# Unread products of the unit matrix on the tensor engine of a two-layer backbone kernel

## The chip, the cores and the metric

The kernel runs on one core of one Trainium2 chip. The metric is the device time of one execution in microseconds (us). The profile shows one execution in the same unit. Engines are named as the profile names them: PE is the tensor engine's product, PEld its weight load, DVE the vector engine, ACT the scalar engine, POOL the GpSimd engine and SP the engine that issues most of the DMAs.

## The reference

Two layers over 1024 latent tokens and 256 context tokens, width 1024, all in fp32. Cut to what matters here:

```python
def reference(x, c, ctx, c_ctx, mod_w, mod_b, norm_g, ...):
    x_lat, x_ctx = x, ctx
    for i in range(DEPTH):                      # DEPTH = 2
        h_lat = rms_norm(x_lat, norm_g[i]) * (1.0 + sc_l) + sh_l
        h_ctx = rms_norm(x_ctx, norm_g[i]) * (1.0 + sc_c) + sh_c
        if i % 2 == 0:   # global GQA with axial rotary | windowed GQA with a sink, each times silu(gate)
            y_lat, y_ctx = even_mixer(...)      # concat(oa * silu(ag), ob * silu(bg)) @ w_out
        else:            # conformer convolution | 2-D neighbourhood attention with a relative bias
            y_lat, y_ctx = odd_mixer(...)       # concat(oc, od * silu(dg)) @ w_out
        x_lat = x_lat + g_l * y_lat
        if i < DEPTH - 1:
            x_ctx = x_ctx + g_c * y_ctx
    return rms_norm(x_lat, final_g)
```

## The kernel before

An fp32 product is made of three products: each operand is split into a high part and a rest (`wh`, `wl`; `hh`, `hl`; `ph`, `pl`), and high times high, rest times high and high times rest are summed in PSUM (L318 to L320). The split's high part is a cast on ACT (L296), the rest a subtraction on POOL or DVE (L299).

Attention of both layers is written in one generator that works through groups of heads and queries, tile by tile. For each tile PE makes the scores `st` (L465, L469), ACT takes their exponential (L477), the split makes `ph` and `pl`, and `flush` adds three products to the group's sum `ov` (L409 to L411). After a group's last tile DVE transposes its denominators (L419), takes their reciprocal (L421), transposes back (L422) and multiplies `ov` by it into `y` (L631 in layer 0, L1367 in layer 1). The maxima that are needed ahead of the exponentials are products into `mx` (L588 in layer 0; L1342 and L1350 in layer 1), reduced on DVE. Layer 1 has 16 groups, eight heads by two halves, and its keys, biases and gates come by DMA.

A root mean square is made in steps by `rstd_steps`: products with ones give the sums of squares `trs` (L251), DVE copies them (`rbv`, L254), POOL makes a first guess (`nr`, L238), DVE refines it (`nt`, `nt`, `nr`, L239 to L241), and PE spreads it over the partitions (`bc`, L261).

The end of layer 1 goes in three parts: part 0 is the first half of the tokens, parts 1 and 2 are quarters. For each part `out1_end` makes the last output products `po` (L318 to L320, for parts 1 and 2 only the last of eight slices of the inner dimension), adds them to `x` (L1435) and sums the squares (ACT L1464, adds on DVE and POOL L1468, L1471); `c0`, `c1`, `c2` run `rstd_steps`; `f0`, `f1`, `f2` run `final_norm`, which copies `bc` (ACT L1479), multiplies `x` by it on DVE (L1486) or on POOL (L1484), and writes out. Part 0 is woven into the last attention groups; the rest runs in the order e1 c1 e2 f1 c2 f2.

PSUM has eight banks, given out by `bank(tag)`: two `pp`, two `mx`, two `st`, one `ov` and one `tr`. A new user of a bank waits until the last reader of the old content is done. What an engine runs in which order isn't written down: a scheduler sets it when the program is built, from priorities, dependencies and its own timeline of the engines. Each engine then runs its list strictly in order.

Of the kernel before, what the change touches and what calls it, by code (L numbers as in the profile page):

```python
# [18 lines left out]
P = 128  # L19
# [32 lines left out]
MWB, WRB = 2, 2  # L52
OHQ = 0
PCB = 3
MODP = ((), (1, 3, 6))
FL = (80, -98)
LAG = (0, 0, 6, 12)
# [30 lines left out]
def tile_kernel(ctx: ExitStack, tc: tile.TileContext, a, out):  # L88
    nc = tc.nc
    VE, SC, GP, PE, SY = nc.vector, nc.scalar, nc.gpsimd, nc.tensor, nc.sync  # L90
# [7 lines left out]
    solo = [True]  # L98
# [4 lines left out]
    def bank(tag, name):  # L103
        if tag == "pp" and solo[0]:
            turn[0] += 1
            tag = ("pp", "mx")[turn[0] // 2 % 2]
        return ps.tile([P, 512], F32, tag=tag, name=name, bufs=BUFS[tag])

    uid = [0]

    def nm(s):
        uid[0] += 1
        return f"{s}_{uid[0]}"
# [130 lines left out]
    def rstd_steps(pool, accs, n, tag, inv=1.0, tr="tr"):  # L244


        nb = n // P
        tr = bank(tr, nm("trs"))
        for b in range(nb):
            for k, acc in enumerate(accs):  # L250
                PE.matmul(tr[:, 2 * b : 2 * b + 2], acc[:, b * P : (b + 1) * P], ones, start=(k == 0),  # L251
                          stop=(k == len(accs) - 1))
        v = pool.tile([P, 8], F32, tag="rbv", name=nm("rbv"), bufs=2)
        VE.tensor_scalar(v[:, :nb], tr[:, 0 : 2 * nb].rearrange("p (b two) -> p b two", two=2)[:, :, 0],  # L254
                         inv, EPS, op0=ALU.mult, op1=ALU.add)
        r = newton_rsqrt(pool, v[:, :nb], nb, "rb")
        yield
        yield
        bc = bank(tag, nm("bc"))
        for b in range(nb):  # L260
            PE.matmul(bc[:, b * P : (b + 1) * P], r[:, b : b + 1].broadcast_to([P, P]), ident, start=True, stop=True)  # L261
        return bc
# [129 lines left out]
    def attn_gen(pool, groups, vshare, look, nexts=None):  # L392

        preps = [g.prep for g in groups]
        items = [(g, t) for g in groups for t in range(len(g.tiles))]
        pend = []
        cnt = [0]

        def flush():
            g, t, ph, pl = pend.pop(0)  # L400
            k, q0, n, _ = g.tiles[t]
            if t == 0:
                g.ov = bank("ov", nm("ov"))
                if g.load_v is not None:
                    g.load_v()
            V = g.v(k)
            last = t == len(g.tiles) - 1
            o = g.ov[:, q0 : q0 + n]
            PE.matmul(o, V[:, 64:192], ph[:, :n], start=(t == 0), stop=False)  # L409
            PE.matmul(g.ov[0:64, q0 : q0 + n], V[:, 0:64], ph[:, :n], start=False, stop=False)  # L410
            pvs.append(PE.matmul(o, V[:, 64:192], pl[:, :n], start=False, stop=(last and g.sink is None)))  # L411
            if last:
                if g.sink is not None:
                    PE.matmul(g.ov, g.skm(), g.QL[0:76, :], start=False, stop=True)
                r1 = pool.tile([P, 8, 32], F32, tag="r1", name=nm("r1"), bufs=1)
                r8 = pool.tile([P, 8], F32, tag="r8", name=nm("r8"), bufs=2)
                rb = pool.tile([P, 256], F32, tag="rb", name=nm("rb"), bufs=1)
                for e in range(2):
                    VE.transpose(r1[e * 64 : (e + 1) * 64].rearrange("p a b -> p (a b)")  # L419
                                 .rearrange("p (a q) -> p a q", a=2), g.den(g.ov[64:128, :], e))  # L420
                VE.reciprocal(r8, r1[:, :, 0])  # L421
                VE.transpose(rb, r8[:, :, None].broadcast_to([P, 8, 32]))  # L422
                g.finish(g.ov, rb)

        for p in preps[:2]:
            next(p)
            yield
        for _ in range(2):
            yield
        for p in preps[:2]:  # L430
            for n_, _ in enumerate(p):
                if n_ % 2:
                    yield
        work = []

        def prepare(x, n):

            while n and work and work[0][0] <= x:
                if next(work[0][1], work) is work:
                    work.pop(0)  # L440
                else:
                    n -= 1

        for gi, g in enumerate(groups):
            g.ids = [gi + 2] if gi + 2 < len(groups) else []
            if nexts is not None and gi in nexts:
                g.ids = nexts[gi]
        for g, t in items[:AHEAD]:
            g.ahead(t)
        for x, (g, t) in enumerate(items):  # L450
            if x + AHEAD < len(items):
                items[x + AHEAD][0].ahead(items[x + AHEAD][1])
            if t == 0:
                g.start()
                while any(p is g.prep for _, p in work):
                    prepare(len(items), 1)
                for k in g.ids:
                    next(preps[k])
                    work.append((x + LEAD[layer[0]], preps[k]))
            rate = g.rate * max(len(work), 1)  # L460
            k, q0, n, extra = g.tiles[t]
            KA, KB = g.k()
            st = bank("st", nm("st"))
            cs = slice(k * P, (k + 1) * P)
            sts.append(PE.matmul(st[:, :n], KA[:, cs], g.QH[:, q0 : q0 + n], start=True, stop=False))  # L465
            if not g.bias:
                for lhs, rhs in extra():
                    PE.matmul(st[:, :n], lhs, rhs, start=False, stop=False)
            PE.matmul(st[:, :n], KB[0:68, cs], g.QL[0:68, q0 : q0 + n], start=False, stop=True)  # L469
            ph = pool.tile([P, 512], F32R, tag="ph", name=nm("ph"), bufs=look + 1)  # L470
            pl = pool.tile([P, 512], F32R, tag="pl", name=nm("pl"), bufs=look + 1)
            pf = pool.tile([P, 512], F32, tag="pf" if layer[0] else "ost", name=nm("pf"), bufs=PFB)
            if g.bias and extra is not None:
                VE.tensor_tensor(pf[:, :n], st[:, :n], extra(), op=ALU.add)
                SC.activation(pf[:, :n], pf[:, :n], AF.Exp)
            else:
                SC.activation(pf[:, :n], st[:, :n], AF.Exp, scale=1.0 if g.bias else SCALE)  # L477
            cnt[0] += 1
            split(pf[:, :n], ph[:, :n], pl[:, :n], "s", "v" if cnt[0] % vshare == 0 else "g")
            pend.append((g, t, ph, pl))  # L480
            if t == len(g.tiles) // 2:
                g.gate()
            if t == len(g.tiles) - 1:
                g.last()
            prepare(x, rate // 2)
            yield
            if len(pend) > look:
                flush()
            prepare(x, rate - rate // 2)
            yield  # L490
        while pend:
            flush()
            yield
# [63 lines left out]
    def group0(u, qb):  # L557
# [12 lines left out]
        def maxes(QH, mp):  # L570
            KA = KAs[u]
            for i2 in range(2):
                mx = bank("mx", nm("mx"))
                for i in range(2):
                    hd = 2 * i2 + i
                    PE.matmul(mx[:, i * 256 : (i + 1) * 256], QH[:, hd * P : (hd + 1) * P], KA[:, 0:256],
                              start=True, stop=True)
                VE.tensor_reduce(mp[:, 2 * i2 : 2 * i2 + 2, 0], mx.rearrange("p (i k) -> p i k", i=2),
                                 axis=AX.X, op=ALU.max)
                yield  # L580
            if qb < 2:
                return
            for hd in range(4):
# [7 lines left out]
                else:  # L591
                    lo, hi = max(qb - 1, 2), min(qb + 2, 10)
                    n = (hi - lo) * P
                    mo = (lo - (qb - 1)) * P
                    mx = bank("mx", nm("mx"))
                    PE.matmul(mx[:, :n], q, KA[:, lo * P : hi * P], start=True, stop=True)
                    VE.tensor_tensor_reduce(out=mx[:, :n], in0=mx[:, :n], in1=bmask[:, mo : mo + n],
# [501 lines left out]
    with ExitStack():  # L1099
# [195 lines left out]
        def group1(gi, hd, hf):  # L1295
# [38 lines left out]
            def maxes(QH, mp):  # L1334
                KA = Ks[hd % len(Ks)][0]
                for b in (1, 2, 0, 3):
                    if b in (1, 0):
                        mx = bank("mx", nm("mx1"))
                        b0 = 1 - b
                        bb = (1, 2) if b else (0, 3)  # L1340
# [106 lines left out]

        def out1_end(k):

            hf, o, n = ENDS[k]  # L1450
            accs = []
            for e in range(DK):
                if k == 0:
                    if e % 2 == 0:
                        w = load_w(wp, a["od_wo"], e * P, 256, 256, WB, dks=range(4, 8))
                    yield from out1((4, 5, 6, 7), e, hf, *w, o, n)
                else:
                    yield from out1((7,), e, hf, *wend[e // 2], o, n)
                x = x2[hf][:, e, o : o + n]
                if k:  # L1460
                    sq = dpool.tile([P, 512], F32, tag="ph" if e in SQ else "pl", name=nm("sq2"), bufs=LOOK1 + 1)[:, :n]
# [172 lines left out]
```

## Time and profile before

| what | before |
|---|---|
| median of 3 runs | 1555.79 us (1553.47 to 1557.76) |
| the profiled execution | 1555.72 us, its span 1553.9 us |
| granted clock of PE, mean over the span | 0.967 |
| matmuls | 6984 |
| longest wait of PE at the end of layer 0 | 5.07 us, ended by `y` (DVE L631) |
| longest waits of PE at 1340 to 1360 us | 3.22 us, ended by a DMA, and 1.82 us |
| last `po` region of layer 1 begins | 1525.72 us |
| last work on DVE ends | 1549.2 us |

The table of the page shows each engine's busy time; the slices show it over the span in forty parts, with the granted clock below; the timeline lists single instructions with the idle time before them and what ended it. The prediction quotes the lines that it uses.

### The profile page before, as it was taken

What the parts mean: (1) busy time and instruction counts of PE and PEld (TensorE: products, weight loads), DVE (VectorE), ACT (ScalarE), POOL (GpSimd) and SP (SyncE); (2) the same over time, 40 slices, a digit from 0 to 9 for tenths busy, and PEclk for the clock granted to TensorE, in tenths of its full rate; (3) what the DMA queues carried; (4) which work ended last, traced back from release to release, by engine and by line L of the source; (5) the groups of instructions that cost most, each with busy time, mean ns of one, the idle gap of its engine ahead of it and who ended that gap; (6) DMA issues with size and microseconds to landing.
All of it is one profiled execution on the core that took longest, in us unless ns stands there. A gap on an engine that the chain in (4) does not pass through costs nothing.

```text
span 1553.9 us, 22052 instructions
## 1 busy us (share of the span) xinstructions
PE 1449.1 (93%) x6984; PEld 1172.3 (75%) x6984; DVE 1123.3 (72%) x2172; ACT 759.8 (49%) x1545; POOL 833.5 (54%) x762
## 2 busy tenths in 40 slices
PE   6989989999999989899999889999999999799995
PEld 1878868887789678678887668888787787687784
DVE  4998898689858666654577677999755457586776
ACT  2721354445454755565455555443434455545563
POOL 1561464555555676675455666664542443545574
PEclk9999999999999999999999999999999999899996
DMA  9548245423441124631111121213456888788623
GB/s 339 194 146 270 79 125 174 147 64 121 151 129 44 54 89 143 207 115 56 42 45 35 68 95 57 80 63 123 158 178 222 272 225 263 221 264 240 192 92 109
DMA packets 185614, 221.01 MB, mean 142 GB/s; under 512 B 17421, under 2 KB 139481, under 8 KB 185497
## 3 DMA queue, kind: packets, MB, share of 16 engines
q1 hardware_dynamic: 178832, 208.03, 43.1%
q10 hardware_dynamic: 6664, 11.57, 2.3%
q8 instruction: 55, 0.90, 0.2%
q14 instruction: 63, 0.51, 0.1%
HBM read 159.51 MB, written 60.03 MB: 141 GB/s over the span
## 4 chain that ended last, share of the span: by engine, by line
PE 67%; DVE 12%; DMA 11%; issue 3%; POOL 3%; ACT 2%; SPq 2%; DVEq 0%; ACTq 0%; POOLq 0%
PE p L320 6%; PE p L318 6%; PE p L319 6%; PE ov L409 4%; PE ov L410 4%; PE ov L411 4%; PE st L465 4%; PE po L318 4%; PE st L469 4%; PE po L319 4%; PE po L320 4%; PE pq L320 2%; PE pq L319 2%; PE pq L318 2%; DMA mw<-in_mod_w_dram 2%
## 5 line engine op out<-in xcount | busy, mean ns | idle before, releaser
L299 POOL TENSOR_TENSOR pl<-pf,ph 128x512 fp32r<-128x512 f32 (+4 forms) x321 | 399.9, 1258 | 270.7 <-ACT ph L296 218.9
L299 POOL TENSOR_TENSOR wl<-wr,wh 128x256 fp32r<-128x256 f32 (+2 forms) x256 | 197.7, 788 | 227.9 <-ACT wh L296 203.3
L477 ACT ACTIVATE pf<-st 128x512 f32<-128x512 f32 x284 | 166.2, 596 | 161.7 <-PE st L469 106.3
L296 ACT CAST ph<-pf 128x512 fp32r<-128x512 f32 (+4 forms) x364 | 209.2, 588 | 25.5 <-PE ov L410 17.6
L296 ACT CAST wh<-wr 128x256 fp32r<-128x256 f32 (+2 forms) x264 | 103.2, 404 | 172.2 <-DMA wr<-in_od_d_dram 39.3
L318 PE MATMUL p<-hh,wh 128*128 128x512 f32 x448 | 177.7, 399 | 3.7 <-DVE spk L299 1.4
L319 PE MATMUL p<-hl,wh 128*128 128x512 f32 x448 | 177.9, 398 | 0.2 <-POOL hl L299 0.2
L320 PE MATMUL p<-hh,wl 128*128 128x512 f32 x448 | 175.2, 399 | 0.1
L465 PE MATMUL st<-QH,KAt 128*128 128x512 f32 (+4 forms) x364 | 144.0, 397 | 19.8 <-ACT pf L477 16.5
L409 PE MATMUL ov<-ph,Vt 128*128 128x512 f32 (+4 forms) x364 | 143.6, 394 | 8.8 <-DVE y L631 6.4
L411 PE MATMUL ov<-pl,Vt 128*128 128x512 f32 (+4 forms) x364 | 143.7, 395 | 3.9 <-POOL pl L299 3.8
L410 PE MATMUL ov<-ph,Vt 128*64 128x512 f32 (+4 forms) x364 | 140.8, 387 | 0.0
L469 PE MATMUL st<-QL,KBt 68*128 68x512 f32 (+4 forms) x364 | 138.2, 388 | 0.8 <-DVE QL L388 0.7
L1116 DVE SCALAR_TENSOR_TENSOR cps<-U,taps,cps 128x512 f32<-128x512 f32 x184 | 124.3, 747 | 0.0
L589 DVE TENSOR_REDUCE mp<-mx 128x1 f32<-128x512 f32 x128 | 85.5, 682 | 33.5 <-PE mx L588 32.7
L219 DVE SCALAR_TENSOR_TENSOR macc<-mw,csil,macc 128x512 f32<-128x512 f32 x107 | 97.5, 929 | 14.0 <-DMA mw<-in_mod_w_dram 13.2
L318 PEld LDWEIGHTS p<-hh,wh 128*128 128x128 f32 x448 | 84.6, 189 | 24.5 <-DVE spk L299 1.6
L465 PEld LDWEIGHTS st<-QH,KAt 128*128 128x128 f32 x364 | 69.8, 192 | 42.5 <-ACT pf L477 25.3
L319 PEld LDWEIGHTS p<-hl,wh 128*128 128x128 f32 x448 | 84.6, 189 | 20.4 <-POOL hl L299 0.6
L320 PEld LDWEIGHTS p<-hh,wl 128*128 128x128 f32 x448 | 84.6, 189 | 20.3 <-POOL wl L299 1.0
L411 PEld LDWEIGHTS ov<-pl,Vt 128*128 128x128 f32 x364 | 71.1, 195 | 28.1 <-POOL pl L299 7.6
L409 PEld LDWEIGHTS ov<-ph,Vt 128*128 128x128 f32 x364 | 71.5, 196 | 24.3 <-issue 7.0
(277 smaller groups left out, 3518.4 us busy)
## 6 DMA issues: line engine op xcount, KB each, us to landing
mw<-in_mod_w_dram SPq DMA_DIRECT2D x34, 512.0 KB, 5.6
bs<-in_d_bs_dram SPq DMA_DIRECT2D x16, 832.0 KB, 7.3
Q<-qs SPq DMA_DIRECT2D x40, 256.0 KB, 2.7
QH<-Q SPq DMA_DIRECT2D x80, 128.0 KB, 2.7
bm<-in_d_bm_dram SPq DMA_DIRECT2D x16, 540.0 KB, 6.1
wr<-in_od_d_dram SPq DMA_DIRECT2D x64, 128.0 KB, 2.6
mw<-in_mod_w_dram SPq DMA_DIRECT2D x28, 256.0 KB, 3.1
wr<-in_ev_qkv_dram SPq DMA_DIRECT2D x32, 192.0 KB, 3.8
```

The lines of the kernel that those rows point to most:

```text
L296: SC.copy(hi, src)
L299: (GP if leng == "g" else VE).tensor_tensor(lo, src, hi.bitcast(F32), op=ALU.subtract)
L318: PE.matmul(o, lh, rh, start=first, stop=False)
L319: PE.matmul(o, lh, rl, start=False, stop=False)
L320: done[0] = PE.matmul(o, ll, rh, start=False, stop=last)
L409: PE.matmul(o, V[:, 64:192], ph[:, :n], start=(t == 0), stop=False)
L410: PE.matmul(g.ov[0:64, q0 : q0 + n], V[:, 0:64], ph[:, :n], start=False, stop=False)
L411: pvs.append(PE.matmul(o, V[:, 64:192], pl[:, :n], start=False, stop=(last and g.sink is None)))
L465: sts.append(PE.matmul(st[:, :n], KA[:, cs], g.QH[:, q0 : q0 + n], start=True, stop=False))
L469: PE.matmul(st[:, :n], KB[0:68, cs], g.QL[0:68, q0 : q0 + n], start=False, stop=True)
L477: SC.activation(pf[:, :n], st[:, :n], AF.Exp, scale=1.0 if g.bias else SCALE)
L1116: VE.scalar_tensor_tensor(pc, uc, w, pc, op0=ALU.mult, op1=ALU.add)
```

## The change

A table `WARM` says ahead of which instruction of a kind how many products are put. Counters go over the tiles' `st`, over the `flush` calls (`ov` ahead of the first product, `pl` ahead of the third), and over the maxima. `turn_over(count, tag)` takes a fresh bank of the given tag and issues `count` products of the unit matrix with itself, 128x512, which nobody reads. From the end of layer 1 on (`ending`), `rstd_steps` has 4 products ahead of its sums for part 0 (`solo` is not yet set), 8 for the others in the bank `ov`, and 6 ahead of `bc`; part 2 of `out1_end` has two for each of its eight slices of output.

```diff
+WARM = {"st": {297: 6, 299: 6}, "ma": {}, "mb": {}, "ov": {243: 18, 251: 6}, "pl": {251: 10}, "m1": {1: 6, 25: 5, 33: 8, 53: 5}}
...
+    seen, ending = {}, [False]
+
+    def warm(kind, n=1):
+
+        seen[kind] = seen.get(kind, 0) + n
+        count = sum(WARM[kind].get(k, 0) for k in range(seen[kind] - n + 1, seen[kind] + 1))
+        turn_over(count)
+
+    def turn_over(count, tag="tr"):
+
+        if count:
+            uid[0] -= 1
+            tr = bank(tag, nm("wm"))
+            for _ in range(count):
+                PE.matmul(tr.rearrange("p (a b) -> p a b", a=4), identr, identr[:, None, :].broadcast_to([P, 4, P]),
+                          start=True, stop=True)
...
+        if ending[0] and not solo[0]:
+            turn_over(4, "tr")
+        elif ending[0]:
+            turn_over(8, "ov")
         tr = bank(tr, nm("trs"))
...
         bc = bank(tag, nm("bc"))
+        if ending[0]:
+            turn_over(6, "tr")
...
             o = g.ov[:, q0 : q0 + n]
+            warm("ov")
             PE.matmul(o, V[:, 64:192], ph[:, :n], start=(t == 0), stop=False)
             PE.matmul(g.ov[0:64, q0 : q0 + n], V[:, 0:64], ph[:, :n], start=False, stop=False)
+            warm("pl")
             pvs.append(PE.matmul(o, V[:, 64:192], pl[:, :n], start=False, stop=(last and g.sink is None)))
...
+            warm("st")
             st = bank("st", nm("st"))
...
                     if b in (1, 0):
+                        warm("m1", 2)
                         mx = bank("mx", nm("mx1"))
...
         def out1_end(k):
+            ending[0] = True
...
                     yield from out1((7,), e, hf, *wend[e // 2], o, n)
+                if k == 2:
+                    turn_over(2, "ov")
```

(The kinds `ma` and `mb`, maxima of layer 0, have calls of the same form and no entries.) 124 products are added, and no instruction of the computation is taken away. The scheduler builds a new order with them. Up to the end of layer 0 the lists of all engines are the same.

At the end of layer 0, PE's list before has the last product of one group (`ov_9297`, tile `pl_9470`) and the first of the next (`ov_9583`) with two pairs of scores between and ahead:

```order
L410 MATMUL ov_9297<-ph_9469,Vt_1259 64x512
L465 MATMUL st_9524<-QH_8863,KAt_5707 128x512 [waits Activation_49]
L469 MATMUL st_9524<-QL_8864,KBt_1258 128x512
L411 MATMUL ov_9297<-pl_9470,Vt_1259 128x512 [waits Pool_49]
L465 MATMUL st_9561<-QH_8863,KAt_5707 128x512 [waits Activation_49]
L469 MATMUL st_9561<-QL_8864,KBt_1258 128x512
L409 MATMUL ov_9583<-ph_9492,Vt_1259 128x512 [waits DVE_49,PE_49]
```

With the change PE's list has there (from behind the same `ov_9297<-ph_9469`; `wm` are the added products):

```order
L124 MATMUL wm_9584<-ident 128x512 x15
L492 MATMUL st_9524<-QH_8863,KAt_5707 128x512 [waits Activation_49]
L496 MATMUL st_9524<-QL_8864,KBt_1258 128x512
L124 MATMUL wm_9584<-ident 128x512
L437 MATMUL ov_9297<-pl_9470,Vt_1259 128x512 [waits Pool_49]
L124 MATMUL wm_9584<-ident 128x512
L492 MATMUL st_9561<-QH_8863,KAt_5707 128x512 [waits Activation_49]
L496 MATMUL st_9561<-QL_8864,KBt_1258 128x512
```

```order
L124 MATMUL wm_9704<-ident 128x512 x4
L492 MATMUL st_9628<-QH_8863,KAt_5707 128x512 [waits Activation_49]
L496 MATMUL st_9628<-QL_8864,KBt_1258 128x512
L124 MATMUL wm_9713<-ident 128x512 [waits PE_49]
L124 MATMUL wm_9713<-ident 128x512 x9
L434 MATMUL ov_9583<-ph_9492,Vt_1259 128x512 [waits DVE_49]
```

Seventeen products now lie ahead of `pl_9470`, seventeen more and two further pairs of scores (`st_9606` and `st_9628`) between it and the next group's first `ov`.

At the end of layer 1, PE's list before has, behind the last group's last product, the spreading `bc` of part 0 and the first `po` of part 1:

```order
L411 MATMUL ov_16094<-pl_16247,Vt_12386 128x512 [waits Pool_49]
L261 MATMUL bc_16336<-ident,nr_16327 128x128 [waits DVE_49]
L261 MATMUL bc_16336<-ident,nr_16327 128x128 x3
L318 MATMUL po_4150_16402<-od_3594_14463,wh_16380 128x256 [waits Activation_49]
L318 MATMUL po_4152_16409<-od_3594_14463,wh_16380 128x256
```

and with the change (`wm_16555` is in the bank of `ov`, and its wait for DVE is that for `y`, which reads `ov_16173`):

```order
L273 MATMUL trs_16400<-ones,sq_4067_16178 128x2
L124 MATMUL wm_16555<-ident 128x512 [waits DVE_49,PE_49]
L124 MATMUL wm_16555<-ident 128x512 x7
L124 MATMUL wm_16421<-ident 128x512 [waits DVE_49]
L124 MATMUL wm_16421<-ident 128x512 x5
L342 MATMUL po_4150_16493<-od_3594_14536,wh_16471 128x256 [waits Activation_49]
L342 MATMUL po_4152_16500<-od_3594_14536,wh_16471 128x256
L124 MATMUL wm_16592<-ident 128x512 [waits PE_49]
```

Fourteen products lie ahead of the first `po`, and `bc` has gone behind the first two slices of output. The pairs of part 2 stand between the slices, and its `po` mix with those of part 1.

POOL's last rows before: the adds of squares, then the `nr` of parts 1 and 2, then the closing multiplications of parts 1 and 2.

```order
L1468 TENSOR_TENSOR sq_4172_16485<-sq_4172_16485,sq_4184_16531 128x256 [waits Activation_49,Pool_49]
L238 TENSOR_TENSOR nr_16471<-rbv_16469,mhalf 128x2 [waits DVE_49]
L238 TENSOR_TENSOR nr_16566<-rbv_16564,mhalf 128x2 [waits DVE_49]
L1484 TENSOR_TENSOR x_3593_14462<-x_3593_14462,bcs_16543 128x256 [waits Activation_49]
L1484 TENSOR_TENSOR x_3593_14462<-x_3593_14462,bcs_16543 128x256 x3
```

With the change:

```order
L256 TENSOR_TENSOR nr_16571<-rbv_16569,mhalf 128x2 [waits DVE_49]
L1502 TENSOR_TENSOR sq_4172_16595<-sq_4172_16595,sq_4184_16659 128x256 [waits Activation_49,Pool_49]
L1518 TENSOR_TENSOR x_3593_14535<-x_3593_14535,bcs_16674 128x256 [waits Activation_49]
L1518 TENSOR_TENSOR x_3593_14535<-x_3593_14535,bcs_16674 128x256 x3
L256 TENSOR_TENSOR nr_16706<-rbv_16704,mhalf 128x2 [waits DVE_49]
```

The `nr` of part 2 has gone from ahead of the four multiplications of part 1 to behind them.

More of the change, by code (lines that the diff above doesn't have):

```diff
@@ L572, in maxes @@
             for i2 in range(2):
+                warm("ma", 2)
                 mx = bank("mx", nm("mx"))
@@ L594, in maxes @@
                     mo = (lo - (qb - 1)) * P
+                    warm("mb")
                     mx = bank("mx", nm("mx"))
```

## The prediction

> **What bounds the kernel now.** The page comes first: which engine is busy, how that and the granted clock of the tensor engine (PE) lie over the span, and what the chain that ended last is made of.
>
> ```profile
> PE 1449.1 (93%) x6984; PEld 1172.3 (75%) x6984; DVE 1123.3 (72%) x2172; ACT 759.8 (49%) x1545; POOL 833.5 (54%) x762
> PE   6989989999999989899999889999999999799995
> PEclk9999999999999999999999999999999999899996
> PE 67%; DVE 12%; DMA 11%; issue 3%; POOL 3%; ACT 2%; SPq 2%; DVEq 0%; ACTq 0%; POOLq 0%
> ```
>
> PE is the bound of nearly the whole span, at nearly full clock; what a product on it costs depends on whether PE has a hole at that place. So the second view is the table of stretches, from the place of the first added product on (columns: length, busy time of PE, weight loads, DVE, ACT and POOL with their counts, granted clock, DMA share, GB/s).
>
> ```profile
> 880.00:900.00 20.00, 13.53 (x51) 9.30 (x49) 12.42 (x21) 13.26 (x24) 12.25 (x11) 0.83 0.01 3
> 920.00:1300.00 380.00, 373.94 (x1773) 304.36 (x1772) 267.55 (x486) 167.62 (x338) 190.91 (x199) 1.00 0.51 161
> 1340.00:1360.00 20.00, 12.87 (x45) 9.99 (x46) 8.67 (x20) 9.58 (x19) 8.83 (x10) 0.66 0.88 214
> 1500.00:1520.00 20.00, 19.64 (x98) 16.23 (x98) 12.95 (x23) 14.06 (x31) 15.94 (x15) 1.00 0.13 41
> 1520.00:1540.00 20.00, 13.70 (x73) 12.40 (x72) 17.22 (x37) 8.61 (x22) 11.13 (x10) 0.74 0.28 105
> ```
>
> Two kinds of place show: full ones at clock 1.00 (380 us with 6 us of holes), where each product must cost its own length, and holes beside a low clock, where one might gain. The timeline of PE at the first hole, the end of layer 0, gives both prices (start, length as modelled, line, operands, idle time before and what ended it).
>
> ```profile
> 880.27 0.39 PE L465 MATMUL st<-QH,KAt 128*128 128x512 f32 x1
> ...
> 880.73 0.40 PE L411 MATMUL ov<-pl,Vt 128*128 128x512 f32 x1
> ...
> 887.01 0.77 PE L409 MATMUL ov<-ph,Vt 128*128 128x512 f32 x1 [5.07 <-DVE y L631]
> ...
> 888.43 0.63 PE L409 MATMUL ov<-ph,Vt 128*128 128x512 f32 x1
> 888.86 0.63 PE L410 MATMUL ov<-ph,Vt 128*64 128x512 f32 x1
> ...
> 891.31 0.39 PE L465 MATMUL st<-QH,KAt 128*128 128x512 f32 x1
> ```
>
> From start to start a 128x512 product takes 0.23 us before the wait (880.27 to 880.73 for two) and 0.43 us behind it (888.43, 888.86), up to 891.3. A slow stretch costs the work in it about half of its length: here 4.30 us from 887.01 to 891.31 for ten products that need 10 x 0.234 = 2.34 at full clock, 1.96 us lost.
>
> [...]
>
> **The change part by part.** It adds 124 products of 128x512 and takes nothing away; 70 come from the table, 54 from the end of layer 1. At full clock they are 124 x 0.234 = 29.0 us, so all depends on how many lie in holes.
>
> *Layer boundary (16+1+1+2+4+10 = 34 products).* 17 of them stand ahead of the last product of the group that ends there, `ov_9297<-pl_9470`, which ran at 880.73: 17 x 0.234 = 4.0 us later. Its follower is a chain on DVE:
>
> ```profile
> 881.17 0.92 DVE L419 STREAM_TRANSPOSE r<-ov 64x256 f32<-64x256 f32 x2 [1.81 <-PE ov L411]
> 882.12 1.27 DVE L239 TENSOR_TENSOR nt<-nr,rbv 128x4 f32<-128x4 f32 x1
> ...
> 883.42 1.19 DVE L240 SCALAR_TENSOR_TENSOR nt<-nt,nr 128x4 f32<-128x4 f32 x1
> ...
> 886.02 0.85 DVE L631 TENSOR_TENSOR y<-ov,rb 64x256 f32<-64x256 f32 x2
> ```
>
> That chain took 5.7 us, from 881.17 to 886.87, because three small operations of a reciprocal root (1.27 and 1.19 us, the third counted at 1.2) stood between its steps. In the changed order they stand ahead of it and run while PE does the 17 products, so the chain needs 2.1 us: it starts near 885.1 and ends near 887.2 instead of 886.9. PE meanwhile has 17 more products and two pairs of `st` (moved forward) ahead of the next `ov`, which starts near 890.3 instead of 887.0, but at full clock and with the two pairs done. By 892 both stand about level, the change two softmax tiles ahead. The next hole is here:
>
> ```profile
> 904.56 0.79 PE L411 MATMUL ov<-pl,Vt 128*128 128x512 f32 x1 [3.17 <-POOL pl L299]
> ...
> 908.14 0.33 PE L320 MATMUL po<-hc,wl 128*128 128x256 f32 x1
> ```
>
> 3.6 us of work at half clock, 1.8 lost. Between the two, ACT and DVE pace the stretch (PE busy 13.53 of 20), so what PE gains at 887 is largely waited away again. Bounds: +1.5 us (the late start carried through) to -3.8 (both losses gone); I take **-1.7**, one of the two.
>
> *The maxima of layer 1, m1 (6, 5, 8, 5 products) and st 297/299 (6+6).* Three holes end in front of them:
>
> ```profile
> 1307.64 0.77 PE L318 MATMUL p<-hh,wh 128*128 128x512 f32 x1 [1.07 <-DVE r L421]
> ...
> 1311.12 0.39 PE L320 MATMUL p<-hh,wl 128*128 128x512 f32 x1
> ...
> 1346.94 0.77 PE L409 MATMUL ov<-ph,Vt 128*128 128x512 f32 x1
> ...
> 1352.82 0.77 PE L1342 MATMUL mx<-KAt,QH 128*128 128x256 f32 x2 [3.22 <-DMA gt<-GD]
> ...
> 1358.88 0.31 PE L411 MATMUL ov<-pl,Vt 128*128 128x320 f32 x1
> ...
> 1446.65 0.50 PE L1342 MATMUL mx<-KAt,QH 128*128 128x256 f32 x2 [2.77 <-DMA KAt<-KD]
> ...
> 1447.48 0.57 PE L318 MATMUL po<-oc,wh 128*128 128x512 f32 x1
> ...
> 1451.13 0.39 PE L318 MATMUL po<-od,wh 128*128 128x512 f32 x1
> ```
>
> At 1307 eight products took 3.48 us where 1.87 would do: 1.6 to gain. The five added ones, 1.17 us, meet a wait of 1.07 and delay it by about 0.3 where their bank comes late: **-1.3** (bounds -1.6 and +1.2, the products fully added). At 1352 the half clock lasts 6.06 us, at most 3.0 to gain; the twenty products, 4.7 us, lie in a wait that a transfer ends, so they cost nothing while it lasts. But the order now has the waiting `mx` ahead of `ov` and `st` work that before ran ahead of the wait, from 1346.94 to where the 3.22 us of idle begin (1349.6), and that then comes behind it: 2.7 us at that slow pace, about 1.4 at full clock. Bounds -3.0 and +2.7; I take **-0.8**, nearer to the loss that the row shows than to nothing gained. The DMA issues on SP keep their order up to the last 150 of 977 rows; there they change places by a few rows, and up to 1 us of a transfer's wait either way lies within these bounds. At 1447 the loss is nine products in 3.65 us for 2.1: -1.5 if the five lie in the 2.77 us wait, +1.2 if they lie behind it; **-0.8**. The six at the first m1 place (1180 us) lie in the stretch with 373.94 of 380 busy: 1.4 us at full price, nothing if the next transfer is waited for anyway; **+0.7**. Four products that belong to the first end part are put at about 1500, where PE is busy 19.64 of 20: **+0.9**. Body together: -1.7 - 1.3 - 0.8 - 0.8 + 0.7 + 0.9 = **-3.0 us**.
>
> *The end of layer 1 (the other 50).* PE, DVE and POOL of before:
>
> ```profile
> 1520.67 0.47 PE L411 MATMUL ov<-pl,Vt 128*128 128x512 f32 x1
> 1523.99 2.08 PE L261 MATMUL bc<-ident,nr 128*128 128x128 f32 x8 [2.85 <-DVE nr L241]
> 1525.72 0.99 PE L318 MATMUL po<-od,wh 128*128 128x256 f32 x3
> ...
> 1529.49 0.28 PE L320 MATMUL po<-od,wl 128*128 128x256 f32 x1
> ```
>
> ```profile
> 1522.89 0.85 DVE L1367 TENSOR_TENSOR y<-ov,rb 64x256 f32<-64x256 f32 x2
> ...
> 1527.44 1.71 DVE L1435 SCALAR_TENSOR_TENSOR x<-po,modT,x 128x256 f32<-128x256 f32 x4
> ...
> 1539.65 0.47 DVE L1435 SCALAR_TENSOR_TENSOR x<-po,modT,x 128x256 f32<-128x256 f32 x1
> ...
> 1544.58 4.60 DVE L1486 SCALAR_TENSOR_TENSOR x<-x,fg,bc 128x256 f32<-128x256 f32 x11
> ```
>
> ```profile
> 1526.83 9.26 POOL L1484 TENSOR_TENSOR x<-x,bcs 128x512 f32<-128x512 f32 x7 [4.71 <-ACT bcs L1479]
> ...
> 1543.35 0.69 POOL L238 TENSOR_TENSOR nr<-rbv,mhalf 128x2 f32<-128x2 f32 x1 [1.90 <-DVE rbv L254]
> 1544.62 3.46 POOL L1484 TENSOR_TENSOR x<-x,bcs 128x256 f32<-128x256 f32 x5 [0.58 <-ACT bcs L1479]
> ```
>
> Now eight products of the kind "ov" and six "tr" stand ahead of the first `po` (before: 1525.72). There is one bank "ov", so the eight can't start until DVE has read it in `y`, 1522.89 to 1523.7, and some 0.5 later in the new order, where the sum of a square goes ahead of the chain and two small operations go behind it: 1524.2. Fourteen products take 3.3 us at full clock (`po` at 1527.5, the first `x` near 1528.4, 1.0 late) and 5.7 with the half clock that lasted to 1529.49 before (`po` near 1529.9, first `x` near 1531.0, 3.6 late). I take the middle, +2.3: the hole ahead of the eight is as long as the 2.85 before, which speaks for cold; the dense run then warms it.
>
> From the first `x` to the last DVE is full (1527.44 to 1540.04), so a late start is kept. One `x` of the closing norm, which lay ahead of the first `x`, now lies among them: +0.7. The pairs of products between the `po` (16 x 0.234 = 3.7 us) and the next eight (1.9) lie beside DVE: PE was busy 13.70 of the 20 us there, so they cost nothing as long as DVE is behind PE; without that cover up to +2. Last, POOL: before, the `nr` of the last part (1543.35) ran ahead of the five `x` that end at 1548.1; now four of these `x`, 4 x 0.69 = 2.8 us, stand ahead of it. The last `bc` and seven `x` on DVE wait for it (0.42 each, of the 4.60 for 11); DVE does its own four meanwhile. Before, that `nr` began 3.3 us behind the last `x` (1540.04); now 2.8 later, less about 0.5 where it would have waited anyway: 5.6, and with its own 0.69, the 0.54 from there to the first closing `x` (1544.58), some 0.9 for `bc` and its copy, and 7 x 0.42, DVE ends about 10.7 us behind the last `x`, for 9.14 before (1549.18): +1.6. The twelve products ahead of the last two `bc` lie in these waits; they may win 0.3 by the clock. The end: 2.3 + 0.7 + 1.6 - 0.3 = **+4.3** (bounds: about +1 with a warm PE and the POOL order hidden, +5.9 with a cold one).
>
> **Sum:** -3.0 + 4.3 = +1.3 us on the profiled 1555.72 (span 1553.9 and 1.8 around it): 1557.0. The median of the runs, 1555.79, is the same within 0.1.
>
> **The rivals.** *The holes are all paid back.* If every filled hole keeps full clock, the body gains 1.96 + 1.8 + 1.3 + 3.0 + 1.5 = 9.6, less 1.6 for the products in full stretches, and the end costs +1 with a warm PE: -7.0, 1548.7. For it: the clock is 0.66 to 0.83 in just those stretches, and products lie ahead of each. Against: at 1352 work was moved behind the wait, and layer boundary and end are paced by DVE, ACT and POOL.
>
> *Slower by the one bank.* The eight "ov" products wait for `y`, and the first `po` waits behind them: with PE cold +3.6, then +0.7 and +1.6 as above, +5.9; the body's fills then only cost their 1.6 in full stretches: +7.5, 1563.2. It decides when the clock is still at half at about 1527. For it: PE was at half clock there before, to 1529.49. Against: fourteen dense products are what warmed it at 891.
>
> *The change does nothing.* The products lie in waits, the half clock moves elsewhere, and work that is moved lies where nobody waits: 1555.7.
>
> [...]
>
> **How the numbers follow.** A difference under 0.3%, 4.7 us, is about what a measurement of this kernel can't tell from none: faster is below 1551.1, slower above 1560.5. Forecast 0.40, own range 1550 to 1562 (0.04 faster, 0.28 within, 0.08 slower). Holes paid back 0.32 (0.28 faster, 0.04 within). Slower by the bank 0.18 (0.17 slower, 0.01 within). Nothing 0.10 (within). Together faster 0.32, same 0.43, slower 0.25. The range 1546.5 to 1563.5 takes in the other cases and leaves out the best bounds of all parts at once and the worst.
>
> **What would show it.** In the changed profile: the granted clock in the stretches 880 to 900 and 1300 to 1320 near 1.00 (the fills work), 1340 to 1360 still under 0.85 (the moved `mx`); the last tile's `y` at the boundary ending within 1 us of 886.9 and the next `ov` near 890.3; at the end the first `po` 2 to 4 us behind `y` where it was 2.0 us behind, then `nr` on POOL behind four `x`. Wrong would be: a first `x` no later against the last `ov` than before, 6.8 us from 1520.67, or a stretch at 1340 to 1360 at full clock with `mx` not later than 1352.8.

## The result, and the profile after

The changed kernel is slower: 1575.81 us (median of 6 runs, 1568.6 to 1579.85) against 1556.36 us for the kernel before (6 runs, 1553.47 to 1558.15), a ratio of 1.0122 with a 95% interval of 1.0105 to 1.014. The profiled execution took 1577.97 us, its span 1576.2. The forecast was 1557.0 with a range up to 1563.5.

The page of the changed kernel, in the rows that the prediction shows of the page before (engines, slices of PE and of its clock, the chain):

```profile
PE 1476.7 (94%) x7108; PEld 1194.2 (76%) x7108; DVE 1127.2 (72%) x2172; ACT 760.6 (48%) x1545; POOL 832.3 (53%) x762
PE   6989999999999989899999999999999998898996
PEclk9899989999999999999999999999999999999998
PE 62%; DVE 16%; DMA 13%; issue 4%; POOL 2%; ACT 2%; SPq 1%; ACTq 0%; DVEq 0%; POOLq 0%
```

PE has 124 matmuls and 27.6 us of busy time more, and its clock is better at the end. But the chain now holds 16% of DVE and 13% of DMA, where it held 12% and 11%: time has gone to waits. The stretches of the changed kernel (length, busy PE, PEld, DVE, ACT, POOL, granted clock, DMA share, GB/s):

```profile
880.00:900.00 20.00, 20.00 (x97) 16.16 (x96) 10.19 (x17) 12.60 (x23) 14.32 (x12) 1.00 0.00 0
900.00:920.00 20.00, 15.33 (x70) 12.17 (x69) 18.53 (x31) 11.55 (x27) 8.96 (x12) 0.83 0.08 21
1300.00:1320.00 20.00, 16.43 (x74) 12.99 (x73) 12.60 (x28) 12.61 (x24) 5.30 (x5) 0.91 0.99 306
1340.00:1360.00 20.00, 15.33 (x68) 11.52 (x68) 10.51 (x25) 11.37 (x23) 9.82 (x11) 0.89 0.85 252
1420.00:1440.00 20.00, 16.70 (x69) 13.30 (x70) 11.02 (x29) 10.87 (x22) 8.73 (x10) 0.83 0.81 237
```

and one stretch of the kernel before that the prediction does not show:

```profile
1420.00:1440.00 20.00, 19.86 (x98) 16.23 (x97) 12.05 (x29) 10.56 (x23) 11.09 (x12) 1.00 0.81 246
```

The fill works where it was put: 880 to 900 is full at clock 1.00 (0.83 before), 1340 to 1360 rose from 0.66 to 0.89. At 900 to 920 the clock is 0.83 and at 1300 to 1320 it is 0.91, both as before. The stretch 1420 to 1440, nearly full and at 1.00 before, is now at 0.83.

Where the time went is seen best by a count that isn't in any view: over the matmuls of a trace, in order of their start, I add the columns that each makes, without the added products, and look up when the changed trace reaches the sum that the trace before has at a given time. All such lags come from single profiles, one of each kernel. The lag so found, in us:

| at, in the trace before | lag of the changed kernel | grown by |
|---|---|---|
| 880, ahead of the change | +1.9 | the same instructions in both: scatter of one execution |
| 920 | +2.5 | +0.6 |
| 1180 | +2.6 | +0.1 |
| 1220 | +5.1 | +2.5 |
| 1300 | +3.8 | -1.3 |
| 1380 | +4.9 | +1.1 |
| 1500 | +14.7 | **+9.8** |
| 1520 | +13.3 | -1.4 |

From the last product of `ov` to the end of the span the kernel before takes 33.3 us, the changed one 42.9: **+9.6**. So two places made the loss, 1380 to 1500, where hardly a product was added, and the end.

### The profile page after: what moved, and what is told of

The parts are those of the page before. It is cut to its first block, busy times and chain, and to the rows that moved or that the text cites. A ratio compares the mean times of both kernels' runs of the same rounds, so it can differ in the third digit from the quotient of the medians.

```text
span 1576.2 us, 22310 instructions
## 1 busy us (share of the span) xinstructions
PE 1476.7 (94%) x7108; PEld 1194.2 (76%) x7108; DVE 1127.2 (72%) x2172; ACT 760.6 (48%) x1545; POOL 832.3 (53%) x762
## 4 chain that ended last, share of the span: by engine, by line
PE 62%; DVE 16%; DMA 13%; issue 4%; POOL 2%; ACT 2%; SPq 1%; ACTq 0%; DVEq 0%; POOLq 0%
PE p L344 6%; PE p L343 6%; PE p L342 6%; PE ov L434 4%; PE ov L435 4%; PE ov L437 4%; PE st L492 4%; PE po L342 3%; PE po L344 3%; PE po L343 3%; PE st L496 3%; DMA mw<-in_mod_w_dram 3%; DVE macc L237 2%; DMA KAt<-KD 2%; PE pq L344 2%
## 5 line engine op out<-in xcount | busy, mean ns | idle before, releaser
L344 PE MATMUL pq<-wh,hl 128*128 128x384 f32 x256 | 86.8, 341 | 0.7 <-DVE hl L334 0.7
```

Of the source, the lines that this page charges most:

```text
L344: done[0] = PE.matmul(o, ll, rh, start=False, stop=last)
```

## The experiments

All ratios are to the kernel before, run beside it on the same chip, with their 95% intervals.

### Which part of the table

The two halves of the change, and the two halves of the table:

```diff
e1_end:      WARM empty
e2_table:    -            ending[0] = True
             -                if k == 2: turn_over(2, "ov")
e3_boundary: as e2, WARM with "ov": {243: 18, 251: 6}, "pl": {251: 10} only
e4_layer1:   as e2, WARM with "st": {297: 6, 299: 6}, "m1": {1: 6, 25: 5, 33: 8, 53: 5} only
```

> Leaves the table empty, keeps the 54 products of the end. Theory (the two traces put side by side): the end costs by itself, whatever lies before it, since its fourteen products stand ahead of the first po and POOL's nr behind four x: from the last ov to the end of DVE 10.9 us more than before, some 8 to 11 us on the time. Rival: the end is late only because the body hands it over in another state, and by itself it costs what was forecast, about 4 us or less.

> Keeps the table's 70 products, leaves out the 54 of the end. Theory: the body loses about 9 to 11 us by itself (in the changed trace the same amount of work on PE is reached 11.4 us later at 1520 than at 880). Rival: most of this lag is one execution's scatter, and the table by itself lies within 3 us of before.

> Only the 34 products at the end of layer 0. Theory: the hole filled there (1.6 us ahead by 900) is waited away again by 920, so between 0 and +2 us. Rival: the warm clock there is kept as a gain, -1.5 to -2; or the new order reaches into layer 1 and costs several us there.

> Only the 36 products ahead of the maxima and scores of layer 1. Theory: these carry the body's loss: +8 to +10 us, with the wait for QH (3.2 us each at about 1310 and 1420) in the trace. Rival: only their own length in full stretches, 36 x 0.234 = 8.4 us at most and about 3 where they lie in waits.

Measured: end alone 1.0046 (1.0026 to 1.0066), some 7 us where 8 to 11 were expected; table alone 1.0099 (1.0056 to 1.0142), some 15 us for 9 to 11; the boundary alone 1.0033 (1.0014 to 1.0053), some 5 us; layer 1 alone 1.0062 (1.0038 to 1.0086), some 10 us. The losses are separate: the end is dear by itself, and so is layer 1. The boundary alone is dearer than the 0 to 2 us expected, though at the boundary its trace shows +0.6 us, as that of the whole change does. Its loss lies further on, as the second rival had it: from 920 to 1520 the lag of its trace grows by 5.6 us.

### The order without the products

A product in layer 1 can cost by its length or because the scheduler makes another order with it. To part these, the products are taken out of the finished program, behind the scheduler, where neither a wait nor a signal hangs on them; each engine's list is otherwise that of the parent kernel, row for row.

```diff
+def drop(nc, which):
+    gone = set()
+    for end, tag, m in wms:
+        sync = m.ins.sync_info
+        if which(end, tag) and not (sync and (sync.on_wait or sync.on_update)):
+            gone.add(m.ins.name)
+    for b in nc.m.functions[0].blocks:
+        b.instructions = [x for x in b.instructions if x.name not in gone]
...
+    drop(nc, lambda end, tag: True)
```

> The order of the change on every engine, word for word, with 84 of its 124 products taken out after the order was made (those that neither wait nor are waited for; 40 stay). Theory 'order': most of the loss stays, a ratio of 1.007 to 1.012, since the transfers of layer 1 are issued in the new order. Rival 'products': the loss falls with the products to a third, a ratio of 1.002 to 1.005.

> The order of the kernel that has the 36 products in layer 1 alone (1.0062 of before), with 26 of them taken out after the order was made. Theory 'order': 1.004 to 1.007, the waits for QH of 2.5 to 3 us near 1390 and 1425 and the late 1380 to 1500 stay. Rival 'products': 26 x 0.234 = 6.1 us less, so 1.001 to 1.003.

> The order of the kernel that has the 54 products of the end alone (1.0046 of before), with 30 of them taken out after the order was made: 24 stay, two or so to a bank. Theory: of the end's loss the part in front of the first po (fourteen products at half clock, 5 us) goes nearly whole, the part that POOL's order makes (3 us) stays: about 1.002. Rival: the order makes all of it, and it stays at 1.004 to 1.005.

Measured: layer 1's order with 10 of 36 products left is 1.0058 (1.0038 to 1.0079), no better than 1.0062 with all. The rival had 1.001 to 1.003, and the interval excludes it. So **in layer 1 the order makes the loss, not the length of the products**. The whole change's order with 40 of 124 is 1.0065 (1.0039 to 1.0091) for 1.0122, just under the expected 1.007 to 1.012; the end's order with 24 of 54 is 1.0017 (0.9992 to 1.0041) for 1.0046. So at the end the products' length seems to count, though these two intervals overlap; by the medians it makes up about half of the 0.57% that the whole kernel wins when products go.

The waits of PE for transfers between 1340 and 1520, in the kernel before (operation, what it waited for, us in total, times, longest):

```profile
PE mx L1342 <- DMA gt<-GD: 3.2, 1, 3.2
PE mx L1342 <- DMA KAt<-KD: 2.8, 1, 2.8
PE mx L1342 <- DMA QH<-QD: 0.5, 1, 0.5
```

In the kernel with layer 1's order and ten products:

```profile
PE mx L1385 <- DMA QH<-QD: 6.8, 3, 3.9
PE mx L1385 <- DMA KAt<-KD: 2.3, 1, 2.3
```

In the whole change:

```profile
PE mx L1372 <- DMA QH<-QD: 6.8, 2, 3.6
PE mx L1372 <- DMA KAt<-KD: 1.6, 1, 1.6
```

In the kernel with only the end's products, whose layer 1 has the old order:

```profile
PE mx L1372 <- DMA gt<-GD: 2.4, 1, 2.4
PE mx L1372 <- DMA QH<-QD: 2.4, 2, 1.2
PE mx L1372 <- DMA KAt<-KD: 1.3, 1, 1.3
```

What grew is the wait for `QH`, the queries of a group. It isn't new: at the same `mx`, near 1412 in the trace before, PE waits 0.5 us before, and between nothing (n1) and 1.89 us (e5) in the others with the old order. In the five kernels with the change's order there it waits 3.19, 1.87, 2.67, 1.78 and 2.58 us (the change, e2, e4, o1, o2), and three of these have a second such wait of 2.1 to 2.9 us near 1381. Behind the waits the clock differs too: from 1380 to 1500 these five spend 3.4 to 10.2 us at half clock, the kernel before 3.4, and the five others with the old order (e1, o3, and n1, e5, e5b, which follow below) none. The growth of lag from 1380 to 1500 agrees: +9.8, +6.8, +10.8, +10.8 and +7.7 us in the five with the change's order, with 124 to 10 products; -0.7, -1.5, +0.4, -1.8 and -2.6 in the five with the old order.

Layer 1's order reaches the end as well. From the last `ov` to the end of the span e2, e4 and o2, which have no product there, take 35.3 to 36.1 us; the kernel before, e3, e5 and e5b take 32.4 to 33.5.

### Whose place on SP it is

DMA issues on SP in the changed kernel, just ahead of the wait at 1422.68 (start, length, line, transfer):

```profile
1401.03 0.45 SPq L1349 DMA_DIRECT2D gt<-GD  x1
1407.23 0.47 SPq L1403 DMA_DIRECT2D O1d<-y  x1
1408.02 0.35 SPq L353 DMA_DIRECT2D wr<-in_od_wo_dram  x1
1409.15 0.33 SPq L1343 DMA_DIRECT2D bs<-in_d_bs_dram  x1
1409.57 0.38 SPq L353 DMA_DIRECT2D wr<-in_od_wo_dram  x1
1410.05 1.33 SPq L385 DMA_DIRECT2D KAt<-KD  x2
1411.43 0.96 SPq L1330 DMA_DIRECT2D QH<-QD  x1
```

and in the kernel before, at the same head:

```profile
1394.95 0.47 SPq L1320 DMA_DIRECT2D gt<-GD  x1
1400.73 0.45 SPq L361 DMA_DIRECT2D KAt<-KD  x1
1403.22 0.46 SPq L1373 DMA_DIRECT2D O1d<-y  x1
1403.74 0.58 SPq L1314 DMA_DIRECT2D bs<-in_d_bs_dram  x1
1404.37 0.45 SPq L361 DMA_DIRECT2D KAt<-KD  x1
1404.85 0.59 SPq L1301 DMA_DIRECT2D QH<-QD  x1
```

Before, one half of the keys was issued ahead of `O1d`, which waits for the last group's `y`. Now both halves, 384 KB each, stand behind it: SP stood still from 1401.5 to 1407.2, then issued two weight loads and the 832 KB of `bs`, and only then the keys and the queries. The last load of `QH` took 10.1 us to land (6.6 before), and PE stood:

```profile
1422.68 0.47 PE L1372 MATMUL mx<-KAt,QH 128*128 128x256 f32 x2 [3.19 <-DMA QH<-QD]
...
1426.05 0.63 PE L496 MATMUL st<-QL,KBt 68*128 68x512 f32 x1
1426.47 0.63 PE L342 MATMUL po<-oc,wh 128*128 128x512 f32 x1
```

Behind the wait the products start 0.42 us apart (1426.05, 1426.47), for 0.24 at 1423.19: the records have half clock from 1424.06 on, for 6.83 us, which costs about half of that, 3.4 us. With the 3.19 us of the wait this is 6.6 of the 9.8 us. Two kernels move the load of the keys:

```diff
+            with later(-100):
                 heads[hd] = load_k(hd, KD[i][ds])
```

in the kernel with layer 1's products (q1) and in the kernel before (q2). On SP the keys then stand ahead of `O1d` and `bs` in q1, and behind `O1d`, `bs` and a `wr` in q2, which has no product.

> The kernel with the 36 products in layer 1 alone (1.0062 of before), and the load of a head's keys (KAt) put on the list with a higher priority: on SP it then stands ahead of O1d, bs and wr, where the change has it behind them. Theory 'transfers': the waits of 2.5 to 3 us for QH near 1390 and 1425 go, and the ratio falls to 1.000 to 1.003. Rival: it isn't the place of these transfers, and the ratio stays at 1.005 to 1.007.

> The kernel before, with no product added at all, and the same higher priority for KAt; the scheduler then makes an order in which one head's KAt stands behind O1d, bs and wr, as in the change. Theory 'transfers': a wait for QH of some 3 us appears at that head and the ratio is 1.002 to 1.006, slower without any product. Rival: with no product the time stays that of before, 0.998 to 1.001.

Measured: q1 1.0043 (1.0021 to 1.0065), outside the expected 1.000 to 1.003, and with an interval that takes in the parent's 1.0062. In its trace the wait at this place is gone (one of 1.1 us for `QH` is left near 1383), and from 1380 to 1500 the lag grows by 2.4 us instead of 10.8; but its end is slow (38.9 us from the last `ov`, for 35.3 in e4 and 33.3 before) though no product is there, since the new order reaches that far. q2 is 1.0014 (0.9986 to 1.0042), which tells neither way; its lag from 1380 to 1500 is -1.4, and what it loses comes at 1300 to 1380 (+3.4). The wait of some 3 us for `QH` that was expected of q2 did not come, though SP has the change's order at that head, with `bs` and a `wr` between `O1d` and the keys:

```profile
1403.05 0.47 SPq L1374 DMA_DIRECT2D O1d<-y  x1
...
1404.81 1.09 SPq L361 DMA_DIRECT2D KAt<-KD  x2
1405.95 0.63 SPq L1302 DMA_DIRECT2D QH<-QD  x1
```

```profile
1415.39 0.39 PE L1343 MATMUL mx<-KAt,QH 128*128 128x256 f32 x2
```

The last load of `QH` took 7.7 us in q2 and landed at 1414.30. In q2's order PE had products of `po` to run until 1415.39, so nothing stood. So whether PE waits depends not only on the place on SP, but also on what else the order gives PE to do there. That the place of these transfers is the cause of the 10 us isn't shown: q1 changed much of the order besides, and q2 has the place without the wait. What is shown is that the order as a whole costs them. One more order, that of e3 and of o4 (further below), gave +0.6 in the one profile and +7.7 in the other: what it costs there also hangs on the execution.

### The end

> The order of the kernel with the products of the end alone (1.0046 of before); of the fourteen ahead of the first po eleven are taken out after the order was made, all others stay. Theory 'fourteen in front': the first po comes back to some 5 to 6 us behind the last ov (10.3 with all), and the ratio to 1.001 to 1.003. Rival 'pairs and order': the later products and POOL's order make the loss, and it stays at 1.004 or more.

The edit is `drop` as above, for the products 4 to 17 in the order of the code (the six of `c0`, the eight of `c1`): 3 of the 14 ahead of the first `po` stay, all others too. Measured: 1.0024 (1.0002 to 1.0046) for 1.0046, and the first `po` 6.3 us behind the last `ov`, for 10.3 with all and 5.05 before. So by the medians about half of the end's loss is the fourteen in front, though the two intervals overlap; the first `po` came back as expected. From the last `ov` to the end of the span, single profiles: 33.3 us before, 41.7 in e1, 38.6 with the eleven gone, 38.0 with thirty gone (o3); some 5 us are left that the order and the remaining products make.

The end of the changed kernel on PE, DVE and POOL:

```profile
1533.31 0.47 PE L437 MATMUL ov<-pl,Vt 128*128 128x512 f32 x1
1535.52 2.11 PE L273 MATMUL trs<-ones,sq 128*128 128x2 f32 x14 [1.73 <-DVE sq L1502]
1537.48 6.25 PE L124 MATMUL wm<-ident 128*128 128x512 f32 x14
1543.57 0.40 PE L342 MATMUL po<-od,wh 128*128 128x256 f32 x2
...
1560.49 2.86 PE L124 MATMUL wm<-ident 128*128 128x512 f32 x6 [1.11 <-DVE rbv L276]
1563.14 1.02 PE L285 MATMUL bc<-ident,nr 128*128 128x128 f32 x4
```

```profile
1539.46 0.16 DVE L259 SCALAR_TENSOR_TENSOR nr<-nt,nr 128x4 f32<-128x4 f32 x1
1544.71 0.88 DVE L1465 SCALAR_TENSOR_TENSOR x<-po,modT,x 128x256 f32<-128x256 f32 x2 [5.09 <-PE po L344]
...
1559.89 0.48 DVE L1465 SCALAR_TENSOR_TENSOR x<-po,modT,x 128x256 f32<-128x256 f32 x1
...
1569.91 2.83 DVE L1520 SCALAR_TENSOR_TENSOR x<-x,fg,bc 128x256 f32<-128x256 f32 x7 [1.21 <-ACT bcs L1513]
```

```profile
1564.65 2.80 POOL L1518 TENSOR_TENSOR x<-x,bcs 128x256 f32<-128x256 f32 x4 [2.74 <-ACT bcs L1513]
1567.41 0.71 POOL L256 TENSOR_TENSOR nr<-rbv,mhalf 128x2 f32<-128x2 f32 x1
```

The fourteen start only when `y` is read (1536.94) and run from 1537.48 to 1543.57, 0.43 us each, all at half clock, and DVE stands 5.09 us for the first slice. Six more wait for `rbv` and then stand ahead of a `bc` whose factor was ready at 1562.3: 0.8 us more. POOL's `nr` comes behind four `x`, as the order said.

### The boundary alone

```diff
e5, e5b:       WARM with "ov": {243: 18} only, no products at the end
o4_boundary18: e3_boundary with drop for the last 16 of its 34 products (3 of these stay)
```

With the eighteen alone, SP's order from 930 us on is that of before, and the other engines' differ in a few neighbouring rows.

> Only the 18 products at the first place of the end of layer 0; the order of layer 1 is then that of before on all engines. Theory: filled hole, warm clock, and given back by 920: a ratio of 0.9995 to 1.0010. Rival 'clock': the 1.9 us of half clock at 887 are kept: 0.998 to 0.999.

> The 18 products at the end of layer 0 alone, measured again in more rounds. Theory 'hole that is filled to its length pays': 2.2 us at the boundary, a ratio of 0.9985 +- 0.001. Rival: given back behind the boundary, 1.0000 +- 0.001.

> The order of the kernel with all 34 products at the end of layer 0 (1.0033 of before), with 13 of the last 16 taken out after the order was made. Theory 'length': the boundary gains again some 2 us in the trace, and the ratio falls by 0.15 to 0.2% to about 1.0015; what is left is the order of layer 1 that came with them. Rival 'order at the boundary': the boundary stays at +0.6 us and the ratio at 1.003.

Measured: 0.9989 (0.9967 to 1.0011) and, in five rounds, 0.998 (0.9961 to 1.0). From 880 to 920 the lag of these two kernels falls by 2.3 and 1.9 us, where all 34 products give +0.6 and seven kernels without any there lie between -0.5 and +1.1. So by the traces eighteen products gain about 2 us, 0.13% of the time, and the ratio agrees with it; but it isn't clear of no change by the first measurement and touches it in the second. PE there, with the eighteen alone:

```profile
886.66 0.39 PE L437 MATMUL ov<-pl,Vt 128*128 128x512 f32 x1
886.89 0.39 PE L124 MATMUL wm<-ident 128*128 128x512 f32 x1
...
889.76 0.47 PE L434 MATMUL ov<-ph,Vt 128*128 128x512 f32 x1 [0.52 <-DVE y L660]
```

and with the whole change:

```profile
886.75 0.39 PE L437 MATMUL ov<-pl,Vt 128*128 128x512 f32 x1
...
890.00 2.46 PE L124 MATMUL wm<-ident 128*128 128x512 f32 x10
892.29 0.40 PE L434 MATMUL ov<-ph,Vt 128*128 128x512 f32 x1
```

With eighteen, `ov` starts as soon as `y` is done, at full clock, 0.52 us after PE ran dry. The sixteen others only hold it up, 3.1 us from `pl` to `ov` against 5.5. In o4, where 13 of them are gone, the boundary gains again (-1.2 us), as theory 'length' had it, but its ratio is 1.0043 (1.0013 to 1.0072) for the expected 1.0015. So the rest of its order, that of layer 1, costs by itself: its lag grows by 5.4 us from 1300 to 1380 and by 7.7 from 1380 to 1500.

## Why the prediction was wrong

*Direction and size.* The sum was -3.0 for the body and +4.3 for the end. The traces give +11.4 for the body (13.3 less the 1.9 that lay ahead of the change) and +9.6 for the end, less what lies in one execution's scatter. Of the rivals "slower by the one bank" came nearest; its price for the end was right in kind and too small, and it had nothing for layer 1. Of the signs that the prediction named, the clock at 880 to 900, the times of `y` and `ov` at the boundary and POOL's `nr` behind four `x` came true. The clock at 1300 to 1320 (0.91, not near 1.00) and at 1340 to 1360 (0.89, not under 0.85) and the first `po` (6.6 us behind `y`, not 2 to 4) did not.

*The step that failed: the new order of layer 1.* The prediction said that the issues on SP change places by a few rows in the last 150 of 977, and that up to 1 us of a transfer's wait lies within the bounds. In layer 1 it priced the rows that were added and, but for the `mx` at 1352, let those that moved stand at nothing. The runs put a loss of about 10 us there (+6.8 to +10.8 against -2.6 to +0.4), with or without the products, in longer waits for `QH` and more time at half clock. Which of the moved rows is to blame stays open. That both halves of `KAt` stand behind `O1d` could be read ahead of the run; what was missing was the question which transfer is the last to land ahead of each `mx`, and what PE has to do until then, in a stretch where the DMA share is 0.8 to 0.9.

*The boundary.* The times were met: `y` and the next `ov` came at 887.6 and 890.2, forecast 887.2 and 890.3, if one takes off the 2.1 us by which the trace was late already (the same product runs at 882.15 and 880.03). The gain of 1.7 wasn't there (+0.6). The seventeen products behind `pl_9470` filled no hole; they delayed `ov`, which started 2.6 us behind the end of `y`. The second hole stayed cold, 0.83 from 900 to 920 in both, and DVE was busy 18.53 us of these 20.

*1180 and 1307.* The six products cost their length: +1.9 to +3.4 us from 1180 to 1220 in the four kernels that have them all there, +0.3 to +1.7 in the others, forecast +0.7. At 1307 no gain is seen: a wait of 3.16 us for `QH` came in front of it, and kernels without the five products there have such waits too (3.88 in e1), so it is not of the products' making.

*1352 and 1447.* At 1352 right in kind: the clock rose (0.89 for 0.66 from 1340 to 1360) and PE gained little, with `mx` waiting 3.60 us behind its transfer. At 1447 the clock rose as well (1.00 for 0.91 from 1440 to 1460); whether that won the 0.8 forecast can't be seen beside the loss there.

*The end.* First `x`: forecast 1.0 to 3.6 us late, taken as 2.3; measured 4.6 (11.4 us behind the last `ov`, 6.8 before), beyond even the cold bound. The one bank, the wait for `y` and the half clock were as told; the clock did not rise halfway through. Choosing the middle between cold and warm was the error, since the row before (half clock at just that place) spoke for cold. The argument on the other side, that fourteen dense products warmed PE at 891, misread the row: ten stood there, in a half-clock stretch that had begun in the wait, at 884.35, and lasted 6.83 us. At the end it began at 1536.70 and lasted 6.83 us too, and all fourteen fell into it. That dense products end such a stretch was the author's estimate; no run shows it. From the first `x` to the last 15.65 us for 12.68: +3.0, forecast +0.7; DVE waited for slices that come later between pairs and `bc`, and the closing `x` lay among them. From the last `x` to the end of DVE 12.4 for 9.1: +3.3, forecast +1.6 and -0.3 for products that were taken as hidden; the six ahead of `bc` were not. These are 10.9 us on DVE; what follows to the end of the span was 1.3 us shorter, which gives the +9.6.

## What to carry to other kernels

Where a scheduler orders the program, an added instruction costs what the order that it makes costs, here more than its own length: compare the lists of the DMA queue first, and ask for each transfer that is waited for what now stands ahead of it, and what the waiting engine has to do until it lands. Products that are to keep the tensor engine's clock up belong ahead of what ends the wait, and no more of them than the hole is long: in the one hole tried (880 to 900, clock 1.00 with eighteen or thirty-four, 0.83 before), eighteen gained 2 us by the traces and thirty-four nothing. A filler in a bank that a waited-for result still occupies can start only when the wait ends (here at 1537.48, 0.54 us behind `y`), and is then in front of the work that it was to help (here 6.1 us, to 1543.57).

## What the runs showed of the hardware

In the changed kernel's records the granted clock is 1.0 or 0.5; of the fifteen stretches at 0.5 ahead of the last one, seven lasted 3.41 us, seven 6.83 and one 10.24. Half clock came with a wait of 3.19 us (1422.68 in the changed kernel, 0.5 from 1424.06 to 1430.88) and with one of 1.07 us (1307.64 in the kernel before, 0.5 from 1307.60 to 1311.02). These stretches shift with the execution: at 406.5 us the kernel before has one of 3.41 us, the changed kernel none near there, with the same instructions. Of the kernels with the same instructions up to 880 us the same sum of work was reached between 1.3 us earlier and 6.6 us later than in the profile of before. Lag ahead of a change is scatter, and only its growth behind can be put down to the change. The waits of layer 1 for transfers scatter too (1.9 to 4.0 us for the same `QH` near 1310), so that a single profile there proves little; five against five did.
